# Two-layer hybrid decoder on one core: channel-mixing pieces made between steps of the u projection, the pool stage one group late, key/value sums in two banks

## The chip, the cores and the metric

The kernel runs on one core of one Trainium2 chip. The metric is the device time of one execution in microseconds (us). The kernel before took 1982.2 us in the median of three runs (1977.94 to 1982.73). One further execution was profiled; all rows of the profile are from that one.

The core has five engines with a queue each: PE does matrix products into PSUM, DVE and ACT work on SBUF and PSUM, POOL on SBUF, and SP issues the transfers (DMA). An engine takes the instructions of its queue in order and waits at one whose inputs or buffers are not ready. The program below is written for a scheduler that simulates the engines when the kernel is compiled: the order of the program is a priority, and the order in a queue can differ from it.

## The reference

```python
for l in range(DEPTH):                                   # 2 layers, x is (1, 1024, 1024)
    h = rms_norm(x, g_pre_mix[l]) * (1.0 + scale_m) + shift_m
    proj = h @ w_in[l] + b_in[l]
    q, k, v, u = jnp.split(proj, [512, 640, 768], axis=-1)
    attn_out = sliding_window_attention_with_sinks(rotary(q), rotary(k), v, sinks[l])
    pool_out = causal_pool_mixer(u, pool_w[l], pool_scale[l])
    mix = jnp.concatenate([attn_out, pool_out], axis=-1) @ w_out[l]
    x = x + gate_m * rms_norm(mix, g_post_mix[l])
    h = rms_norm(x, g_pre_ffn[l]) * (1.0 + scale_f) + shift_f
    f = (jax.nn.silu(h @ w_gate[l]) * (h @ w_up[l])) @ w_down[l]
    x = x + gate_f * rms_norm(f, g_post_ffn[l])

def causal_pool_mixer(u, ...):       # four groups of 128 channels, windows 2, 4, 8, 16
    pooled = trailing_mean(u_group, w) - u_group
    out_group = (pooled @ pool_w[group]) * pool_scale
```

The shifts, scales and gates come from a small projection of `c`. All data are float32.

## The kernel before, in words

**Numbers as two parts.** Each operand of a product is split into a rounded part hi and a rest lo (`split`, line 211: hi on ACT at L213, lo on DVE at L214), and each product is three matmuls, hi hi, hi lo, lo hi (`mm3`, line 238: L239, L242, L243). One has up to 128 x 128 x 512.

**Halves and passes.** The 1024 tokens are worked in two halves of 512 (four tiles of 128). For each half three passes read the normalised input, eight channel pieces of 128 kept transposed as hi and lo in eight `hT` buffers: `q_pass` (line 653; four PSUM banks, one per token tile), `kv_pass` (line 617; keys and values, 256 columns per token tile) and `u_pass` (line 674; the pool mixer's input, four banks, one per channel group). Each step of a pass loads a strip of `w_in` into a `raw` buffer (`weight`, line 216), splits it and issues twelve products (of 256 columns in `kv_pass`, which loads one strip for two k). When a pass ends, its banks are emptied: q on DVE (L672), key/value on DVE (L651), u on ACT (L686). There are four accumulator banks (`acc`), three others (`msc`) for transposes and short products, and one for attention (`pv`).

**Pieces.** `pre_norm_piece` (line 494) makes one channel piece: four transposes of 128 x 128 on PE into an `msc` bank (L489), scale and shift on ACT into `raw` (L475), if wanted a write of that to memory (`keep`, L498, on SP's queue), then the split into an `hT` buffer.

**Rings.** `part` (line 124) hands out buffers in pieces of 512 columns: `raw` is two tiles of 2048, `hi` and `lo` three tiles of 1024 each, so four and six pieces of 512. A tile is free again only when everything that reads any of its pieces is done.

**Order of the work.** Stages are generators, and `run` (line 596) drives one of them and, after each of its steps, advances others by a share of calls:

```python
for _ in stream:
    i += 1
    for o in others:
        while o[2] * steps < o[1] * i:
            o[2] += 1
            next(o[0], None)
```

Per layer the order is: `dense0` (q and key/value of the first half); then `dense` (line 1339), 20 steps: u of the first half (8 steps, which also make the pieces of the second half), key/value of the second half (4 steps), q of the second half (8 steps), with the attention of the first half, `pool0` (line 1344: eight empty calls, then the pool stage of the first half) and a part of the small projection beside it; then the output projection of the first half (`mix_out`), which begins with the four pool groups; then `post_norm` of the first half, whose normalised rows `fn` are the input of the channel mixing; then u of the second half (line 1358) with ten calls of attention; then, at line 1362, the eight pieces of the first half for the channel mixing, each written to memory too (`kept0`, read again much later by `up_sums`); then `up_firsts` (line 1002), the first products of the channel mixing, whose weights come through `operand` (line 1009, loads at L1012), with attention and the pool stage of the second half beside it (line 1373). The first of each two matmul groups there uses the first four pieces, the second the other four.

**Pool stage.** `pool_mix` (line 890) takes one group per call: one to four doubling sums on DVE (L903), the scaled difference (L907), for the first half a correction of the first 16 columns (L912, L913), a split, three matmuls with the group's weights `pwh` and `pwl` into an `msc` bank, and the scaling on ACT into `cat` (L920).

**Key/value banks.** With `pairs` given (the very first pass of the kernel only), two token tiles share a bank; in the other three passes each of the four token tiles has a bank of its own. With two in a bank, only the first product of the first tile clears the bank, and only the last of the second closes it; `other` keeps the second tile's opening product behind the first tile's.

## Time and profile before

| what | value |
|---|---|
| median of three runs | 1982.2 us (1977.94 to 1982.73) |
| the profiled execution's own time | 1979.58 us |
| its span, first to last instruction | 1977.8 us |
| instructions | 26045 |
| mean granted clock of PE | 0.985 |
| HBM traffic over the span | 169 GB/s |

In the rows of the profile, `out<-in` names the buffers that an instruction writes and reads, `x` is a count, and times are us from the span's start. A group's row ends with busy us, the mean ns of one, and the idle time of the engine just before, with what ended it. In the timeline a row is start, length, engine, line and operation, and in brackets the idle time before it and its releaser. PEld is the loading of PE's weights, which runs beside its matmuls; SPq is the issue of a transfer. A matmul's row shows its whole latency, so rows overlap; matmuls of 256 columns start about 0.12 us apart, those of 512 columns about 0.23.

### The profile page before, as it was taken

To read this page: it belongs to the slowest core of one execution; us is meant where nothing else is said; L and a number is where in the kernel's file an instruction comes from. 1 tells how busy PE (TensorE), PEld (TensorE's weight loads), DVE (VectorE), ACT (ScalarE), POOL (GpSimd) and SP (SyncE) were. 2 spreads that over 40 slices of the span, in tenths; PEclk is the share of its full clock that TensorE was granted. 3 is DMA by queue.
4 is the path that set the end of the run, shared out by engine and by line. 5 is a ranking of instruction groups with operands and counts; after the bars stand their busy time and mean duration, and the time that the engine had idled before them with its cause. 6 is when DMAs were issued, how large, how long until landed. Compare 5 with 4: busy or idle time off the path is not lost. (4 is left out here: it accounts for less than half of the span.)

```text
span 1977.8 us, 26045 instructions
## 1 busy us (share of the span) xinstructions
PE 1891.2 (96%) x8958; PEld 1551.3 (78%) x8958; DVE 1564.9 (79%) x2907; ACT 957.1 (48%) x1794; POOL 49.7 (3%) x100
## 2 busy tenths in 40 slices
PE   6989989999999999999999899899999999999997
PEld 4877768887888887778887777788778888878886
DVE  6988976679889886787878889656788898767687
ACT  4775785653222223445648658845522222335452
POOL 1000000010000000000000000000200000000000
PEclk9999989999999999999999899899999999999999
DMA  9236553555455446842556455445555554474343
GB/s 327 88 108 187 176 192 121 160 192 192 157 180 192 161 164 229 302 129 88 178 192 182 131 146 184 135 131 189 176 192 176 175 177 170 142 262 171 112 134 112
DMA packets 222052, 336.62 MB, mean 170 GB/s; under 512 B 16696, under 2 KB 120008, under 8 KB 221920
## 3 DMA queue, kind: packets, MB, share of 16 engines
q1 hardware_dynamic: 221776, 334.92, 51.2%
q8 instruction: 70, 1.15, 0.2%
q14 instruction: 62, 0.51, 0.1%
q0 software_dynamic: 32, 0.00, 0.0%
q10 hardware_dynamic: 112, 0.04, 0.0%
HBM read 262.00 MB, written 72.89 MB: 169 GB/s over the span
## 5 line engine op out<-in xcount | busy, mean ns | idle before, releaser
L213 ACT ACTIVATE hi<-raw 128x1024 fp32r<-128x1024 f32 (+1 forms) x388 | 332.0, 867 | 335.7 <-PE acc L242 214.5
L214 DVE TENSOR_TENSOR lo<-raw,hi 128x1024 fp32r<-128x1024 f32 (+1 forms) x388 | 379.7, 984 | 80.6 <-ACT hi L213 77.1
L239 PE MATMUL acc<-t,hi 128*128 128x512 f32 x704 | 276.1, 392 | 4.9 <-ACT hi L213 4.9
L243 PE MATMUL acc<-t,lo 128*128 128x512 f32 x704 | 275.9, 393 | 3.6 <-DVE lo L214 3.6
L242 PE MATMUL acc<-t,hi 128*128 128x512 f32 x704 | 275.5, 391 | 0.0
L243 PE MATMUL acc<-bh,lo 128*128 128x512 f32 x528 | 207.1, 392 | 0.0
L239 PE MATMUL acc<-bh,hi 128*128 128x512 f32 x528 | 203.9, 391 | 3.0 <-ACT bh L213 3.0
L239 PE MATMUL acc<-hT,hi 128*128 128x512 f32 x480 | 192.0, 400 | 9.7 <-ACT hi L213 9.1
L1061 DVE TENSOR_TENSOR fn<-acc,fn 128x512 f32<-128x512 f32 x220 | 150.4, 684 | 50.9 <-PE acc L243 50.1
L242 PE MATMUL acc<-hT,hi 128*128 128x512 f32 x480 | 189.7, 395 | 0.0
L243 PE MATMUL acc<-hT,lo 128*128 128x512 f32 x480 | 187.8, 394 | 0.0
L239 PEld LDWEIGHTS acc<-t,hi 128*128 128x128 f32 x704 | 133.3, 189 | 34.1 <-ACT hi L213 6.5
L243 PEld LDWEIGHTS acc<-t,lo 128*128 128x128 f32 x704 | 133.1, 189 | 34.2 <-DVE lo L214 6.7
L242 PEld LDWEIGHTS acc<-t,hi 128*128 128x128 f32 x704 | 133.2, 189 | 27.8
L242 PE MATMUL acc<-ph,hi 128*128 128x512 f32 x320 | 126.4, 395 | 0.7 <-DVE ph L214 0.6
L239 PEld LDWEIGHTS acc<-bh,hi 128*128 128x128 f32 x528 | 99.4, 189 | 24.8 <-ACT bh L213 3.8
L273 DVE SCALAR_TENSOR_TENSOR ada<-ar,c_act,ada 128x512 f32<-128x512 f32 x140 | 104.4, 746 | 15.9 <-DMA ar<-in_ada_w_dram 14.9
L243 PEld LDWEIGHTS acc<-bh,lo 128*128 128x128 f32 x528 | 100.1, 190 | 20.7
L239 PEld LDWEIGHTS acc<-hT,hi 128*128 128x128 f32 x480 | 91.3, 190 | 29.9 <-ACT hi L213 10.8
L999 ACT ACTIVATE fn<-fn 128x512 f32<-128x512 f32 x44 | 27.8, 633 | 168.4 <-DVE fn L1061 157.9
L243 PEld LDWEIGHTS acc<-hT,lo 128*128 128x128 f32 x480 | 90.7, 189 | 18.7 <-DVE lo L214 0.4
L242 PEld LDWEIGHTS acc<-hT,hi 128*128 128x128 f32 x480 | 91.5, 191 | 17.4
(302 smaller groups left out, 3877.1 us busy)
## 6 DMA issues: line engine op xcount, KB each, us to landing
ar<-in_ada_w_dram SPq DMA_DIRECT2D x160, 256.0 KB
raw<-in_w_gate_dram SPq DMA_DIRECT2D x44, 512.0 KB
raw<-in_w_up_dram SPq DMA_DIRECT2D x44, 512.0 KB
raw<-in_w_in_dram SPq DMA_DIRECT2D x80, 256.0 KB
raw<-keeps SPq DMA_DIRECT2D x40, 512.0 KB
keeps<-fn SPq DMA_DIRECT2D x66, 256.0 KB
two_b<-in_w_down_dram SPq DMA_DIRECT2D x30, 512.0 KB
raw<-keepa SPq DMA_DIRECT2D x25, 512.0 KB
```

The lines of the kernel that those rows point to most:

```text
L213: nc.scalar.activation(hi, src, AF.Copy)
L214: nc.vector.tensor_sub(lo, src, hi.bitcast(F32))
L239: ins = nc.tensor.matmul(dst, lh, rh, start=first, stop=False)
L242: nc.tensor.matmul(dst, lh, rl, start=False, stop=False)
L243: return nc.tensor.matmul(dst, ll, rh, start=False, stop=last)
L273: nc.vector.scalar_tensor_tensor(acc, w, c_act[:, i : i + 1], acc, op0=ALU.mult, op1=ALU.add)
L999: nc.scalar.activation(g, g, AF.Silu)
L1061: nc.vector.tensor_add(halves_of(dst)[m], bank, halves_of(src)[m])
```

## The change

Three edits, all in the order of the work; no instruction's operation or size changes.

1. `kv_pass`: two accumulator banks in all passes, two token tiles to a bank, in the way that the first pass of the kernel had already.
2. `pool_mix`: the matmuls and the scaling of a group are issued in the call after the one that makes its split; the last group has a call of its own, so the stage has five calls. `pool0` gets 13 calls over the 20 steps of `dense` in place of 20: its eight empty ones come by step 11, its five working ones at steps 13, 14, 16, 17 and 19 (before: steps 9 to 12).
3. The eight pieces of the first half for the channel mixing come from a generator beside the u pass of the second half: three empty calls, then one piece per call. Five pieces are asked for behind u's steps 4 to 8, the other three behind the pass.

```diff
     def kv_pass(l, hT, par, qkvs, pairs=None):
-        if pairs:
-            dsts = [pairs[t // 2][:, t % 2 * 256 : t % 2 * 256 + 256] for t in range(NT)]
-        else:
-            dsts = [acc_bank()[:, :256] for _ in range(NT)]
+        banks = pairs or [acc_bank() for _ in range(2)]
+        dsts = [banks[t // 2][:, t % 2 * 256 : t % 2 * 256 + 256] for t in range(NT)]
...
-                first, second = pairs and t % 2 == 0, pairs and t % 2 == 1
+                first, second = t % 2 == 0, t % 2 == 1
...
-    POOL_STEPS = len(WINDOWS)
+    POOL_STEPS = len(WINDOWS) + 1
...
+        def mapped(g, hi, lo_):
+            bank = msc_bank()
+            sl = slice(g * P, (g + 1) * P)
+            mm3(bank, pwh[:, sl], pwl[:, sl], hi, lo_, True, True)
+            sc = cols[:, 8 * KD + g : 8 * KD + g + 1]
+            nc.scalar.activation(cat[:, g, :], bank, AF.Copy, scale=sc)
+
+        late = None
         for g, w in enumerate(WINDOWS):
...
             hi, lo_ = part("hi"), part("lo")
             split(hi, lo_, pooled)
-            bank = msc_bank()
-            sl = slice(g * P, (g + 1) * P)
-            mm3(bank, pwh[:, sl], pwl[:, sl], hi, lo_, True, True)
-            sc = cols[:, 8 * KD + g : 8 * KD + g + 1]
-            nc.scalar.activation(cat[:, g, :], bank, AF.Copy, scale=sc)
+            if late:
+                mapped(*late)
+            late = (g, hi, lo_)
             yield
+        mapped(*late)
+        yield
...
-        run(dense(), 2 * KD + 4, (att, ATT_STEPS + 2), (pool0(), 2 * KD + 4), (side, 16))
+        run(dense(), 2 * KD + 4, (att, ATT_STEPS + 2), (pool0(), KD + POOL_STEPS), (side, 16))
...
-        run(u_pass(l, 1, pieces, cols, uts[1], lambda k, ins: None), KD, (att, 10))
+        kept0 = dr.tile([KD, P, T], F32, tag="h0", name="h0", bufs=DEPTH)
+        hts0 = []
+
+        def first_half():
+            for _ in range(3):
+                yield
+            for k in range(KD):
+                hts0.append(pre_norm_piece(0, k, par["abf"], None, fn, kept0[k]))
+                yield
+
+        pre = first_half()
+        run(u_pass(l, 1, pieces, cols, uts[1], lambda k, ins: None), KD, (att, 10), (pre, KD))
         pool = pool_mix(l, 1, uts[1], cols, cats[1][1])
-
-        kept0 = dr.tile([KD, P, T], F32, tag="h0", name="h0", bufs=DEPTH)
-        hts0 = [pre_norm_piece(0, k, par["abf"], None, fn, kept0[k]) for k in range(KD)]
+        drain(pre)
         ops = {B11: hts0[:HK], B21: hts0[HK:]}
```

## The prediction

> **What bounds the kernel now.** I read the page first, then windows set by stage, the waits, the groups by form, and the timeline of the two places that the diff touches.

> ```profile
> span 1977.8 us, 26045 instructions
> PE 1891.2 (96%) x8958; PEld 1551.3 (78%) x8958; DVE 1564.9 (79%) x2907; ACT 957.1 (48%) x1794; POOL 49.7 (3%) x100
> ```

> PE is busy for 96% of the span, so only stretches in which PE is not full, or its clock is low, can give anything. 1977.8 - 1891.2 = 86.6 us are idle in all. The next view gives the stretches that the change touches: per stretch its length, then the busy time of PE, PEld, DVE, ACT and POOL, the granted clock, and the DMA share.

> ```profile
> core 0: us, PE busy (x) PEld busy (x) DVE busy (x) ACT busy (x) POOL busy (x), PEclk, DMA share, GB/s
> 130.00:148.00 18.00, 12.85 (x63) 9.36 (x62) 13.52 (x39) 10.07 (x25) 0.00 (x0) 0.91 0.00 1
> 148.00:178.00 30.00, 29.72 (x166) 24.92 (x166) 25.57 (x68) 16.29 (x44) 1.09 (x4) 1.00 0.64 193
> 260.00:271.50 11.50, 11.50 (x67) 9.82 (x67) 6.11 (x22) 8.78 (x22) 0.88 (x5) 1.00 0.02 5
> 271.50:288.06 16.56, 10.40 (x67) 8.17 (x65) 10.82 (x30) 14.66 (x31) 0.33 (x1) 0.88 0.67 213
> 288.06:294.30 6.24, 6.24 (x17) 4.95 (x18) 4.68 (x6) 3.73 (x7) 0.00 (x0) 0.51 0.87 266
> 310.00:320.00 10.00, 10.00 (x46) 8.24 (x45) 8.11 (x11) 4.30 (x6) 0.00 (x0) 1.00 0.48 155
> 1103.00:1124.00 21.00, 15.54 (x72) 11.56 (x71) 16.89 (x44) 10.91 (x28) 0.47 (x2) 0.83 0.43 127
> 1124.00:1156.00 32.00, 31.99 (x170) 26.90 (x169) 25.72 (x70) 16.01 (x43) 1.35 (x4) 0.95 0.47 139
> 1250.00:1266.58 16.58, 10.85 (x67) 8.46 (x65) 10.80 (x30) 14.65 (x31) 0.33 (x1) 0.81 0.66 215
> 1266.58:1270.40 3.82, 3.82 (x12) 3.04 (x13) 3.64 (x6) 3.52 (x7) 0.00 (x0) 0.50 0.79 248
> ```

> Two kinds of hole, each once per layer. I count a hole as PE's idle time plus what the low clock takes, busy x (1 - clock).
> **Hole A** lies between the u projection of the second half and the first matmul of the channel mixing: layer 0 6.16 + 10.40 x 0.12 = 7.4, then 6.24 x 0.49 = 3.1; layer 1 5.73 + 10.85 x 0.19 = 7.8, then 3.82 x 0.50 = 1.9. Together 20.2 us.
> **Hole B** lies between the key/value pass and the q pass of the second half: layer 0 5.15 + 12.85 x 0.09 = 6.3; layer 1 5.46 + 15.54 x 0.17 = 8.1. Together 14.4 us.
> So 34.6 us (1.7%) is the most that this change can take away. Behind both holes PE is full again (29.72 of 30.00, 31.99 of 32.00).

> **Hole A, the pieces.** The timeline of layer 0 in order:

> ```profile
> 251.33 0.33 SPq L223 DMA_DIRECT2D raw<-in_w_in_dram  x1
> 251.71 1.90 SPq L510 DMA_DIRECT2D cfa<-in_x_dram  x4
> 258.43 2.19 ACT L463 ACTIVATE fn<-fn,rs 128x1024 f32<-128x1024 f32 x2 [0.23 <-DVE rs L257]
> 273.17 1.04 PE L489 MATMUL msc<-ident,fn 128*128 128x128 f32 x8
> 274.66 3.36 SPq L498 DMA_DIRECT2D h<-raw  x4
> 280.57 0.38 SPq L1012 DMA_DIRECT2D raw<-in_w_gate_dram  x1
> 282.81 0.46 SPq L1012 DMA_DIRECT2D raw<-in_w_up_dram  x1
> 286.95 1.06 ACT L213 ACTIVATE hi<-raw 128x1024 fp32r<-128x1024 f32 x1 [0.96 <-DMA raw<-in_w_up_dram]
> 288.06 0.80 PE L239 MATMUL acc<-hT,hi 128*128 128x512 f32 x1 [1.70 <-ACT hi L213]
> ```

> The groups by form in 271.50 to 288.06 (count | busy us, mean ns of one | idle before):

> ```profile
> L475 ACT ACTIVATE raw<-msc,colp 128x512 f32<-128x512 f32 x8 | 5.8, 790 | 0.0
> L214 DVE TENSOR_TENSOR hT<-raw,hT 128x512 fp32r<-128x512 f32 x8 | 5.2, 688 | 3.3 <-ACT hT L213 3.3
> L213 ACT ACTIVATE hT<-raw 128x512 fp32r<-128x512 f32 x8 | 4.7, 649 | 0.0
> ```

> The normalised rows are there at 258.43 + 2.19 = 260.6, yet the first transpose runs at 273.17: in program order all eight pieces stand behind the u pass. Then ACT paces them, 0.79 + 0.65 = 1.44 us a piece, 11.5 for eight; it is busy 14.66 of 16.56 us. The last link is a transfer: the first weights of the channel mixing are issued at 280.57 and 282.81, since their buffer (the `raw` ring, two tiles of 2048) has to be given back by the first four pieces' keep writes, which start at 274.66. They are there at 286.95, and PE starts at 288.06.

> What the change does here: per layer 32 transposes (0.13 us each, 1.04 / 8), 16 ACT operations, 8 DVE operations and 8 keep writes on SP's queue move, none is added. Three of u's eight steps pass before the first piece, five pieces are made behind steps 4 to 8, three behind the pass. Nothing can start before 260.6, so the pieces get the last 11 us of the u pass. The 20 transposes put 20 x 0.13 = 2.6 us into a stretch where PE is full (11.50 of 11.50); they delay u by that and leave the hole by the same amount: 0. DVE has room for 8 x 0.69 = 5.5 (6.11 of 11.50 busy): 0. ACT is the limit: it has 11.50 - 8.78 = 2.7 us free ahead of 271.5 and 16.56 - 14.66 = 1.9 behind it. If all ACT work that stands ahead of the first weight split stays ahead of it, that split moves up by at most 4.6 us. If it overtakes the four pieces that only the second matmul group needs (4 x 1.44 = 5.8), the transfer decides, and the whole 7.4 could go. Below nothing: ACT's attention work may be pushed back by a piece at each step (1.44 x 5 = 7.2 lost), which I leave at the end of the bounds because ACT's free time covers most of it. I take 4.6 per layer, 9.2 for both; layer 1 has the same ACT figure (14.65 of 16.58).
> The clock's part of the hole is 1.25 + 3.06 + 2.06 + 1.91 = 8.3 us. No row shows the clock with a shorter hole; its ends are 0 and 8.3, and I take half, 4.1. Hole A gives **13.3**.
> [...]

> The queue that the pieces are moved past is SP's: the keep of piece 0 now stands in program order ahead of u's weight loads 4 to 7, that of piece 1 ahead of 5 to 7, and so on. I cost that at 0, because the queue's order is not the program's: the last load of u's weights went out at 251.33 and the second half's residual, which the program asks for only after the whole next stage, at 251.71, both long before the first keep (274.66). The scheduler sends a load as soon as its buffer is free. What it costs if that cover is gone is the third rival.

> **Hole B, the pool stage and the banks.**

> ```profile
> 129.80 0.28 PE L242 MATMUL acc<-lo,hT 128*128 128x256 f32 x1
> 129.92 0.28 PE L243 MATMUL acc<-hi,hT 128*128 128x256 f32 x1
> 132.11 0.51 PE L239 MATMUL msc<-hi,pwh 128*128 128x512 f32 x1 [1.91 <-ACT hi L213]
> 137.90 0.69 DVE L903 TENSOR_TENSOR pt<-pt 128x513 f32<-128x513 f32 x1
> 138.50 0.42 DVE L651 TENSOR_TENSOR qkv<-acc,bqkv 128x256 f32<-128x256 f32 x1
> 138.97 0.50 PE L239 MATMUL acc<-hi,hT 128*128 128x512 f32 x1 [1.29 <-DVE qkv L651]
> 140.17 0.50 PE L242 MATMUL acc<-lo,hT 128*128 128x512 f32 x1 [0.69 <-DVE lo L214]
> ```

> The pool stage's groups by form in 104 to 148:

> ```profile
> L903 DVE TENSOR_TENSOR pt<-uT 128x527 f32<-128x527 f32 x4 | 2.8, 697 | 0.0
> L214 DVE TENSOR_TENSOR lo<-pt,hi 128x512 fp32r<-128x512 f32 x4 | 2.7, 686 | 1.0 <-ACT hi L213 1.0
> L907 DVE SCALAR_TENSOR_TENSOR pt<-pt,uT 128x512 f32<-128x512 f32 x4 | 2.7, 682 | 0.0
> ```

> The key/value pass ends at 129.92. PE then waits 1.91 us for a pool group's split, and at 138.97 for the last key/value eviction (L651), which stands behind the pool sums in DVE's line; at 140.17 for a weight split on the same engine. All three waits are DVE's backlog. The pool stage is ten doubling sums (1 + 2 + 3 + 4 by the loop) of about 0.70, four of 0.68 and four splits of 0.69: 12.5 us of DVE.
> The change moves it from steps 9 to 12 of this run, on top of the key/value pass, to steps 13, 14, 16, 17 and 19, inside the q pass (13 calls over 20 steps, the first eight empty); maps each group one call later, so that PE meets a split made a call ago; and leaves two banks free in the key/value pass, so that the first two of four token tiles of q need no eviction at all. Instructions are the same in number.
> The DVE work does not go away. PE's hole closes only as far as DVE works in what are now its own pauses: 18.00 - 13.52 = 4.5 and 21.00 - 16.89 = 4.1 us in the two holes, 8.6 together, while the upper end is the whole hole, 14.4. The q pass behind has DVE pauses of 4.4 (30.00 - 25.57) and 6.3 (32.00 - 25.72), so 12.5 us of pool work fit only with the hole's own time; that is why I stay at DVE's figure, **8.6**. The lower end: a pool group's hi and lo halves are held a call longer in a ring of six halves, so a weight split can wait as at 132.11, 1.91 at each of eight groups, 15.3 lost. I take 0 for it, since about four halves are asked for between two calls (one for a weight at each step, three for attention in four).
> The third key/value pass (layer 1, first half) and the pool stage of the second half: 0. The first waits for q's first bank either way; the second lies under the channel mixing's matmuls, where PE is full (10.00 of 10.00 from 310), and would cost one 1.91 a group if that cover were gone.
> [...]

> **Sum.** 9.2 + 4.1 + 8.6 = 21.9 us off the profiled execution's 1979.6 (span 1977.8 and 1.8 around it): 1957.7. That execution lies 2.6 below the median of the runs, 1982.2, so the forecast against the runs is **1960**.

> **Rivals.** All against 1982.2; 0.3% (5.9 us) is about what a measurement of this kernel can tell from no change.
> *Only one hole closes.* For it: both holes have a second limiter close behind (ACT 14.66 of 16.56; DVE 25.57 of 30.00). Hole A alone gives 1969, hole B alone 1974. Chance 0.21.
> *Hidden anyway, no change.* The pieces cannot start before 260.6, and if the scheduler already orders ACT by readiness, the first weight split may stay where it is, while hole B moves with the pool sums into the q pass and opens there. Holes return elsewhere: 1979 to 1985. Chance 0.14.
> *Keeps ahead of weight loads, slower.* If the schedule keeps the new program order on SP, a load of u's weights waits for a keep, the keep for ACT, ACT for the transposes, and these for the u step before. Then each step shows a load (282.81 to 286.95, 4.1 us) and a split (1.06): 5.2 us of bare PE, four steps a layer, 41.6 in all, 1982.2 - 21.9 + 41.6 = 2002. It decides from three steps a layer on (31.2 against 21.9); with one or two caught the change still wins. Against it stand the rows at 251.33 and 251.71. Chance 0.10.
> The forecast keeps 0.55. Faster: 0.55 + 0.21 = 0.76; within 0.3%: 0.14; slower: 0.10.
> **Range.** Both holes gone in full gives 1982.2 - 34.6 = 1947.6; hole B at its lower end with hole A as forecast gives 1982.2 - 13.3 + 15.3 = 1984. I take 1947 to 1983, which leaves out the slow rival and little else; the likeliest case's own range is 1948 to 1972.

> **What would show it.** Right: transposes `msc<-ident,fn` between u's matmuls from about 11 us ahead of u's end; fewer than 16.6 us from u's last matmul to the first of the channel mixing, about 12; the clock above 0.9 there; no L651 ahead of q's first matmul; pool matmuls among q's, with no wait on a split. Wrong: `raw<-in_w_in` issues behind `h<-raw` and PE waiting on `hi` inside the u pass (the slow rival); a DVE wait of the same length later in the q pass or at the start of the output projection (hidden anyway).

## The result and the profile after

The changed kernel takes **1947.07 us** in the median of four runs (1944.55 to 1948.14), against 1981.39 (1977.94 to 1982.73) for the kernel before: a ratio of 0.9828 with a 95% interval of 0.9811 to 0.9845, or 34 us less. The forecast was 1960 in a range of 1947 to 1983. The sign and the places were right; the gain was 34 us where 22 were forecast. The median lies 0.07 us inside the lower end of the range, and two of the four runs lie below it, so that it fell inside is luck. The profiled execution took 1944.55 us (before 1979.58), at a mean granted clock of 0.993 (before 0.985).

The head of the page after the change:

```profile
span 1942.8 us, 26040 instructions
PE 1874.0 (96%) x8958; PEld 1541.0 (79%) x8958; DVE 1564.3 (81%) x2907; ACT 954.5 (49%) x1794; POOL 49.0 (3%) x100
```

DVE's work is the same to 0.6 us (1564.9 before), and PE has the same 8958 matmuls: no work was taken away. PE is idle for 68.8 us instead of 86.6, and its same matmuls are busy for 17.2 us less, most of which is the clock (1891.2 x 0.015 = 28.4 us lost to it before, 1874.0 x 0.007 = 13.1 after). The windows by stage of the changed kernel (length, then busy time of PE, PEld, DVE, ACT and POOL, the clock, DMA), the counterparts of the ones in the prediction:

```profile
126.30:144.30 18.00, 18.00 (x114) 15.32 (x113) 16.82 (x51) 12.09 (x30) 0.47 (x2) 1.00 0.35 111
144.30:170.00 25.70, 23.36 (x125) 18.76 (x124) 25.04 (x66) 15.65 (x42) 1.14 (x4) 1.00 0.48 146
252.40:269.90 17.50, 17.46 (x111) 14.94 (x111) 12.02 (x38) 15.55 (x34) 0.89 (x5) 1.00 0.42 148
269.90:275.37 5.47, 3.47 (x27) 2.86 (x25) 4.10 (x12) 5.47 (x10) 0.00 (x0) 0.97 0.82 249
275.37:281.60 6.23, 6.23 (x28) 5.30 (x29) 4.62 (x12) 5.35 (x17) 0.33 (x1) 0.75 0.71 232
1083.90:1101.00 17.10, 16.86 (x104) 14.34 (x104) 16.54 (x50) 10.30 (x26) 0.41 (x2) 1.00 0.58 162
1226.50:1231.90 5.40, 3.40 (x27) 2.79 (x25) 4.02 (x12) 5.40 (x10) 0.00 (x0) 1.00 0.87 266
1231.90:1236.00 4.10, 4.10 (x22) 3.40 (x23) 3.71 (x10) 4.10 (x14) 0.33 (x1) 1.00 0.51 178
```

Hole B is gone: the 18 us behind the key/value pass hold 18.00 us of PE work at full clock, where they held 12.85 at 0.91. Hole A is 5.5 us long in both layers where it was 16.8, and of these PE is idle for 2.0. By the prediction's own count (idle time plus what the clock takes), hole A fell from 20.2 us to 2.00 + 0.10 + 1.56 in layer 0 and 2.00 in layer 1, 5.7 in all, and hole B from 14.4 to 0.2. Not all of that is gain: from the key/value pass to q's end PE was idle for 7.5 + 5.5 us before and is still idle for 3.3 + 1.9, now mostly within the q pass (rows below).

The waits of PE in layer 0's key/value and q passes (104 to 180 us), the two longest of each, first before, then after (us in total, times, longest):

```profile
PE msc L239 <- ACT hi L213: 1.9, 1, 1.9
PE acc L239 <- DVE qkv L651: 1.3, 1, 1.3
```

```profile
PE acc L242 <- DVE lo L214: 1.9, 2, 1.5
PE msc L737 <- DVE rt L705: 1.3, 1, 1.3
```

The wait for a pool group's split and that for the last key/value eviction (L651, which is L649 now) are gone. Two other waits on DVE are the longest now: on weight splits inside the q pass (1.46 us ahead of 150.23 and 0.42 ahead of 158.05), and on L705 behind it (1.33 ahead of 174.10).

What is left of hole A, in the timeline of the changed kernel:

```profile
267.89 0.38 SPq L1019 DMA_DIRECT2D raw<-in_w_gate_dram  x1
268.88 0.43 SPq L1019 DMA_DIRECT2D raw<-in_w_up_dram  x1
270.14 1.25 PE L489 MATMUL msc<-ident,fn 128*128 128x128 f32 x10
272.24 2.47 SPq L498 DMA_DIRECT2D h<-raw  x3
274.22 1.09 ACT L213 ACTIVATE hi<-raw 128x1024 fp32r<-128x1024 f32 x1
275.37 0.80 PE L239 MATMUL acc<-hT,hi 128*128 128x512 f32 x1 [2.00 <-ACT hi L213]
```

Of the 32 transposes only ten run behind the u pass (before: all 32; 22 run inside it now, the first of them 17.4 us ahead of its end), and the first weights of the channel mixing are issued at 267.89, 2.0 us before the u pass's last matmul (269.91), where it was 9.3 us behind it. The first weight split at 274.22 has no wait of its own ahead of it in this view; ACT is busy for 5.47 of 5.47 us.

Stage by stage, from the first and last matmuls of each in the two traces: from the key/value pass's first to q's last matmul 69.84 to 61.58 in layer 0 and 68.14 to 59.05 in layer 1 (17.4 saved); from u's first matmul to the channel mixing's first 47.75 to 41.09 and 47.74 to 41.07 (13.3 saved); layer 0's channel mixing 2.7 saved; the third key/value pass (layer 1, first half) 13.71 to 11.39 (2.3 saved); all else 0.6 lost. The sum is the 35.0 us by which the span is shorter.

### The profile page after: what moved, and what is told of

Read it like the earlier page. It is cut to its first block, busy times and chain, and to the rows that moved or that the text cites. A ratio compares the mean times of both kernels' runs of the same rounds, so it can differ in the third digit from the quotient of the medians.

```text
span 1942.8 us, 26040 instructions
## 1 busy us (share of the span) xinstructions
PE 1874.0 (96%) x8958; PEld 1541.0 (79%) x8958; DVE 1564.3 (81%) x2907; ACT 954.5 (49%) x1794; POOL 49.0 (3%) x100
## 5 line engine op out<-in xcount | busy, mean ns | idle before, releaser
L213 ACT ACTIVATE hi<-raw 128x1024 fp32r<-128x1024 f32 (+1 forms) x388 | 332.5, 869 | 377.8 <-PE acc L242 220.7
L214 DVE TENSOR_TENSOR lo<-raw,hi 128x1024 fp32r<-128x1024 f32 (+1 forms) x388 | 382.9, 993 | 113.4 <-ACT hi L213 112.6
L239 PE MATMUL acc<-t,hi 128*128 128x512 f32 x704 | 276.7, 393 | 5.7 <-ACT hi L213 5.7
L243 PE MATMUL acc<-t,lo 128*128 128x512 f32 x704 | 276.1, 393 | 3.4 <-DVE lo L214 3.4
L242 PE MATMUL acc<-t,hi 128*128 128x512 f32 x704 | 276.0, 392 | 0.0
L243 PE MATMUL acc<-bh,lo 128*128 128x512 f32 x528 | 206.4, 391 | 0.0
L239 PE MATMUL acc<-bh,hi 128*128 128x512 f32 x528 | 203.5, 390 | 3.0 <-ACT bh L213 3.0
L239 PE MATMUL acc<-hT,hi 128*128 128x512 f32 x480 | 191.2, 398 | 7.8 <-ACT hi L213 7.2
L242 PE MATMUL acc<-hT,hi 128*128 128x512 f32 x480 | 188.3, 392 | 0.0
L243 PE MATMUL acc<-hT,lo 128*128 128x512 f32 x480 | 186.8, 393 | 0.9 <-DVE lo L214 0.9
L239 PEld LDWEIGHTS acc<-t,hi 128*128 128x128 f32 x704 | 133.5, 190 | 34.9 <-ACT hi L213 7.3
L243 PEld LDWEIGHTS acc<-t,lo 128*128 128x128 f32 x704 | 133.4, 190 | 34.2 <-DVE lo L214 6.5
L242 PEld LDWEIGHTS acc<-t,hi 128*128 128x128 f32 x704 | 133.5, 190 | 27.9
L242 PE MATMUL acc<-ph,hi 128*128 128x512 f32 x320 | 126.0, 394 | 1.3 <-DVE ph L214 1.1
L239 PEld LDWEIGHTS acc<-bh,hi 128*128 128x128 f32 x528 | 99.1, 188 | 24.6 <-ACT bh L213 3.8
L273 DVE SCALAR_TENSOR_TENSOR ada<-ar,c_act,ada 128x512 f32<-128x512 f32 x140 | 104.7, 748 | 17.0 <-DMA ar<-in_ada_w_dram 15.8
L243 PEld LDWEIGHTS acc<-bh,lo 128*128 128x128 f32 x528 | 99.6, 189 | 20.5
L239 PEld LDWEIGHTS acc<-hT,hi 128*128 128x128 f32 x480 | 90.7, 189 | 27.4 <-ACT hi L213 9.1
L243 PEld LDWEIGHTS acc<-hT,lo 128*128 128x128 f32 x480 | 90.1, 188 | 19.5 <-DVE lo L214 1.3
L242 PEld LDWEIGHTS acc<-hT,hi 128*128 128x128 f32 x480 | 90.7, 189 | 17.3 <-issue 0.2
```

Source lines behind the costliest of these rows:

```text
L213: nc.scalar.activation(hi, src, AF.Copy)
L214: nc.vector.tensor_sub(lo, src, hi.bitcast(F32))
L239: ins = nc.tensor.matmul(dst, lh, rh, start=first, stop=False)
L242: nc.tensor.matmul(dst, lh, rl, start=False, stop=False)
L243: return nc.tensor.matmul(dst, ll, rh, start=False, stop=last)
L273: nc.vector.scalar_tensor_tensor(acc, w, c_act[:, i : i + 1], acc, op0=ALU.mult, op1=ALU.add)
```

## The experiments

Each ratio is against the kernel before, run on the same chip, with its 95% interval. The expectations write TensorE for PE, VectorE for DVE and ScalarE for ACT. The lengths in the table are from each kernel's trace, in us: "kv to q" from the second half's first key/value matmul to the last of q, "u to mixing" from u's first matmul to the channel mixing's first, in layers 0 and 1, and "hole" its last part, behind u's last matmul.

| kernel | median | ratio | kv to q | u to mixing | hole | third kv pass |
|---|---|---|---|---|---|---|
| before | | | 69.84, 68.14 | 47.75, 47.74 | 16.76, 16.79 | 13.71 |
| after | 1947.07 | 0.9828 | 61.58, 59.05 | 41.09, 41.07 | 5.45, 5.47 | 11.39 |
| pieces alone | 1966.11 | 0.9928 [0.9908, 0.9949] | 67.44, 68.04 | 41.08, 41.07 | 5.48, 5.46 | 13.22 |
| pool alone | 1962.35 | 0.9907 [0.9885, 0.9929] | 62.98, 58.73 | 47.13, 47.49 | 16.08, 16.54 | 12.74 |
| banks alone | 1972.36 | 0.9963 [0.9949, 0.9977] | 70.16, 63.87 | 47.72, 47.19 | 16.69, 16.23 | 11.41 |
| pool and banks | 1959.52 | 0.9895 [0.9873, 0.9917] | 61.53, 58.82 | 47.77, 47.28 | 16.82, 16.32 | 11.39 |
| pool: later calls only | 1968.30 | 0.9931 [0.9910, 0.9952] | 58.58, 57.87 | 47.58, 47.63 | 16.67, 16.71 | 13.28 |
| pool: lag only | 1977.78 | 0.9985 [0.9972, 0.9999] | 72.93, 63.37 | 47.34, 47.62 | 16.32, 16.68 | 12.85 |
| six sums left out | 1966.08 | 0.9932 [0.9915, 0.9950] | 63.10, 59.51 | 47.41, 47.36 | 16.41, 16.36 | 12.87 |
| matmuls among transposes | 1981.85 | 1.0007 [0.9994, 1.0020] | 69.89, 67.36 | 48.00, 50.13 | 17.06, 19.20 | 15.10 |
| before, other row buffers | 1961.89 | 0.9913 [0.9889, 0.9937] | 67.74, 66.52 | 37.06, 36.64 | 5.65, 5.65 | 14.86 |
| after, other row buffers | 1943.60 | 0.9812 [0.9787, 0.9836] | 61.36, 58.82 | 35.46, 35.68 | 2.66, 2.65 | 11.39 |
| after, loads behind keeps | 1960.33 | 0.9898 [0.9877, 0.9918] | 63.78, 60.40 | 43.82, 44.15 | 1.43, 1.42 | 11.40 |
| after, weights first | 1942.50 | 0.9810 [0.9785, 0.9836] | 61.96, 58.85 | 36.88, 36.87 | 1.24, 1.25 | 11.39 |

**The three edits by themselves.** The first kernel is the one before with the pieces' generator, the second with the pool stage's lag and its 13 calls, the third with the two banks, the fourth with pool stage and banks; each takes its lines of the diff above as they are.

> The kernel before with the channel pieces' edit alone. By the milestones of the two traces (from the end of the q pass to the first products of the channel mixing, and the stretch behind it) this edit is worth 5.3 + 2.7 us in layer 0 and 7.6 + 0.3 in layer 1. Theory 1, the two holes are separate and add up: 15 to 17 us faster than before (ratio about 0.992), the first channel-mixing matmul about 5.5 us behind u's last instead of 16.8 in both layers, and nothing changed between the key/value pass and the q pass. Rival, the gain behind u is partly a gain of the stages before, handed on: under 10 us.

> The kernel before with the pool stage's edit alone (first half's calls at steps 13 to 19, mapping one call late); key/value products keep four banks. Theory 1, the hole before q is VectorE's backlog of pool sums: 13 to 17 us faster, the matmul of the first pool group moves behind q's first, and the wait on L651 in layer 0 shrinks since the eviction no longer stands behind pool sums. Rival, the hole is the wait for the key/value evictions because the q pass needs the same banks: under 6 us faster, PE still waits for a key/value eviction after the key/value pass.

> The kernel before with the two banks' edit alone. Theory 1 (backlog): the two free banks let q's first steps start while the pool sums still hold VectorE, but the weight splits are in the same line, so 2 to 6 us faster, of which 2.3 in the first half's pass of layer 1. Rival (evictions): 10 us or more faster. Second rival, sharing a bank makes the first tile's eviction wait for the second's matmuls: 0 to 1 us slower.

> The kernel before with the pool stage's and the two banks' edits, without the pieces'. Theory 1, the holes add up: 18 to 20 us faster, so that with the pieces' edit alone it makes up the 34.3 us of the whole change within 3. Rival, pool stage and banks remove the same wait: no more than the better one of the two alone. Second rival, they need each other: more than the sum of the two alone by over 3 us.

Pieces alone give 0.72%, 14.3 us, a little under the expected 15 to 17, and pool with banks 1.05%, 20.8 us; together that is 35.1, the 34.1 of the whole change within the intervals. So the gains at the two holes are separate and add up. (Against expectation kv to q, which the pieces don't touch, is 2.4 us shorter in layer 0 with them, though only 0.1 in layer 1; untouched stages shift by such amounts between these kernels, and no cause is claimed for them.) Inside hole B the pool stage does most (18.4 us alone, above the 13 to 17 expected). Pool stage and banks don't add up: alone they give 18.4 + 7.3 = 25.7, together 20.8. That is 2.4 more than the pool stage alone, with overlapping intervals, so the times don't tell it from the rival by which both remove the same wait; the third key/value pass, 12.74 with the pool stage and 11.39 with both, is where the traces show the banks. The banks alone gave 7.3 us, above the 2 to 6 expected and below the rival's 10, though the interval (4.6 to 10.1) touches both. Their timeline in layer 0 shows why they don't open hole B by themselves:

```profile
132.16 0.51 PE L239 MATMUL msc<-hi,pwh 128*128 128x512 f32 x1 [2.36 <-ACT hi L213]
140.00 0.50 PE L239 MATMUL acc<-hi,hT 128*128 128x512 f32 x1 [1.29 <-DVE qkv L649]
141.21 0.50 PE L242 MATMUL acc<-lo,hT 128*128 128x512 f32 x1 [0.70 <-DVE lo L214]
```

The same three waits as before: q's last token tile still needs the last eviction, and that still stands behind the pool sums in DVE's line. What the banks gave lies in the third key/value pass (2.3 us, in every kernel that has the edit) and in layer 1 from key/value to q (4.3 us). The windows of that q pass, behind q's fifth matmul, before and with the banks alone:

```profile
1114.83:1153.51 38.68, 37.08 (x184) 30.72 (x185) 28.75 (x77) 22.92 (x61) 1.35 (x4) 0.89 0.48 141
```

```profile
1114.41:1148.03 33.62, 33.42 (x182) 27.70 (x181) 27.88 (x75) 20.16 (x56) 0.86 (x4) 0.97 0.53 158
```

37.08 x 0.11 = 4.1 us went to the low clock before, 33.42 x 0.03 = 1.0 here: some 3 us of that stage's gain are the clock, which fell behind the hole in one and barely in the other.

**Which half of the pool edit.** The fifth kernel has only the later calls, the sixth only the lag:

```diff
-        run(dense(), 2 * KD + 4, (att, ATT_STEPS + 2), (pool0(), 2 * KD + 4), (side, 16))
+        run(dense(), 2 * KD + 4, (att, ATT_STEPS + 2), (pool0(), KD + POOL_STEPS), (side, 16))
```

```diff
-            bank = msc_bank()
...
+            if late:
+                mapped(*late)
+            late = (g, hi, lo_)
             yield
+        mapped(*late)
+        yield
```

> The kernel before, and of the pool stage's edit only the later calls: 12 calls over the 20 steps, so the stage starts at step 13 instead of 9; each group is still mapped in its own call. Theory 1, the hole before q is VectorE's backlog and closes because the pool sums leave the key/value pass: 13 to 17 us faster, almost all of the 18.2 that the whole pool edit gave, the fifth matmul of q about 7 us earlier in each layer. Rival, the call's lag is what counts (TensorE no longer meets a split that has just been asked for): under 6 us faster, with waits of about 1.9 us on a pool group's split inside the q pass.

> The kernel before, and of the pool stage's edit only the lag: each group mapped one call after its sums, the calls where they were (steps 9 to 12, the last mapping at step 13). Theory 1 (backlog): 0 to 5 us faster, at most the two waits of 1.9 on a pool group's split per layer; q's fifth matmul moves by under 3 us per layer. Rival (the lag is what counts): 10 us or more.

The later calls alone give 0.69%, 13.7 us, the lag alone 0.15%, 3 us. It is the place of the sums that counts. The lag seems to have its worth on top, some 5 us by intervals that overlap, at another place: with the later calls alone kv to q is even shorter (58.58, 57.87), but from q's last to u's first matmul it takes 67.55 and 69.34 us against 63.24 and 65.33 before; with the lag too that stretch is 63.52 and 64.61. The likely reason: 12 calls over 20 steps put the groups at steps 14, 16, 17 and 19 (not from 13 on, as expected), 13 calls at 13, 14, 16 and 17, so that less of the pool stage is left for the output projection, which needs it first. That was not tried by itself.

**Is it DVE's backlog?** The seventh kernel makes the queue shorter and moves nothing:

```diff
-            while width < w:
+            while width < 2:
```

> The kernel before with six of the ten doubling sums of each pool stage left out (each group makes one; the wider pooling windows are thereby not computed). Nothing else moves. Theory 1 (backlog): six sums of 0.70 us are 4.2 us less VectorE work in front of the weight splits and evictions, so q's fifth matmul comes 3.5 to 4.5 us earlier in each layer, 7 to 9 us in all; the second half's stage, under a full TensorE, gives 0. Rival (evictions or banks, not backlog): under 2 us in all.

0.68%, 13.5 us, nearly twice the 7 to 9 expected, and far from the rival's 2. Key/value to q, one row per layer, before, after, and with the six sums left out:

```profile
107.24:177.08 69.84, 62.34 (x379) 52.32 (x377) 59.50 (x163) 42.90 (x112) 2.29 (x8) 0.98 0.44 134
1085.37:1153.51 68.14, 62.66 (x371) 53.42 (x370) 57.18 (x155) 40.17 (x105) 2.35 (x7) 0.92 0.43 130
```

```profile
108.08:169.66 61.58, 58.30 (x379) 50.45 (x377) 58.66 (x163) 42.41 (x112) 2.35 (x8) 1.00 0.49 152
1067.37:1126.42 59.05, 57.20 (x372) 50.02 (x371) 56.04 (x156) 39.62 (x105) 2.10 (x7) 1.00 0.47 141
```

```profile
107.56:170.66 63.10, 60.32 (x378) 51.11 (x377) 55.76 (x157) 42.80 (x112) 2.19 (x8) 1.00 0.49 147
1079.92:1139.43 59.51, 58.25 (x372) 49.83 (x370) 53.67 (x150) 39.28 (x105) 2.12 (x7) 1.00 0.50 151
```

Read the fourth number, DVE. Left out were 3.7 and 3.5 us of it, and the stretches are 6.7 and 8.6 us shorter. Most of the rest is what a hole costs besides itself: before, the clock took 62.34 x 0.02 + 62.66 x 0.08 = 6.3 us here, and it is whole in both other kernels. In the changed kernel DVE does nearly the same work as before (114.7 us against 116.7), and it is its pauses that went: 69.84 - 59.50 + 68.14 - 57.18 = 21.3 us before, 2.9 + 3.0 = 5.9 after. That is 15.4 of the 17.4 us. Every stretch is an engine's work plus its pauses; that DVE is the engine to count here is what this kernel shows, which takes only DVE work away, together with the fifth, which only moves it. In the changed kernel DVE is busy for 95% of both stretches, and PE for 95 and 97%.

**The clock in hole A.** The eighth kernel asks what the clock does when PE is kept busy there: it adds four ordinary matmuls per piece into the bank that the transposes then overwrite:

```diff
+            bank = msc_bank()
+            hot = pieces[KD - 1][0]
+            for _ in range(4):
+                nc.tensor.matmul(bank, ident_r, hot if k < KD - 1 else hts0[0][0], start=True, stop=True)
+            transposed(0, k, None, fn, bank)
```

> The kernel before with 32 more ordinary 128x512 matmuls per layer, four ahead of each piece's four transposes, into the bank that these then overwrite (0.23 us each, 7.4 us per layer, in a stretch where TensorE is idle for 6 us). [...]

Over 289.50 to 295.70 us, the first 6.2 us of the channel mixing, the clock is 0.72, where before it was 0.51 over the first 6.24, and the time lies between 1.2 us less and 4.0 more. Its windows in layer 0:

```profile
274.00:285.06 11.06, 11.06 (x68) 9.25 (x67) 5.26 (x11) 9.67 (x15) 0.00 (x0) 1.00 0.50 174
286.90:289.40 2.50, 0.03 (x2) 0.01 (x1) 0.87 (x4) 1.11 (x2) 0.00 (x0) 1.00 1.09 375
290.88:294.80 3.92, 3.92 (x17) 3.45 (x17) 2.19 (x9) 2.76 (x10) 0.33 (x1) 0.58 0.80 236
```

With PE full (11.06 of 11.06 us) the clock is 1.00 through all the pieces. Then comes a bare wait of 2.5 us for the first weights, and it falls all the same, to 0.58 some 1.5 us into the products. The time is no shorter; the hole ends behind the same transfer, and in layer 1 it is even 2.4 us longer. What the transposes alone do is not told by this kernel, whose added matmuls filled the pauses too; the trace of the kernel before tells more. Its stretches of halved clock start whole multiples of 3.41 us apart, and last 3.41, 6.83 or 10.24 us but for the one that ends the trace. These are three slots of that length in hole A, counted on from those starts, then the pieces' transposes alone (L489; busy time of PE and PEld) in the first:

```profile
277.15:280.56 3.41, 2.34 (x15) 1.62 (x16) 1.29 (x2) 3.41 (x7) 0.00 (x0) 1.00 0.70 234
280.56:283.97 3.41, 0.94 (x7) 0.50 (x5) 3.30 (x10) 3.41 (x9) 0.00 (x0) 1.00 0.99 329
283.97:287.39 3.42, 2.02 (x6) 1.43 (x6) 2.48 (x9) 2.46 (x10) 0.33 (x1) 0.50 0.96 266
```

```profile
277.15:280.56 3.41, 1.88 (x12) 1.17 (x12) 1.00 0.70 234
```

The first slot has 2.34 us of PE work, of which 1.88 are transposes, and the clock behind it stays at 1.00. The second has 0.94 us (0.66 of it transposes of the attention, L816), and behind it the clock is 0.50. In the traces of the kernel before and of the changed one, between the first 20 and the last 15 us, every slot at full clock with under 1.45 us of PE work (seven, 0.32 to 1.43 us) is followed by a halved one. Without the transposes of L489 four slots of the trace before would be under 1.45 too: from 24.56, 273.73, 277.15 and 1253.36 us on PE is busy for 1.96, 2.88, 2.34 and 3.15 us, of which 1.09, 2.09, 1.88 and 2.55 are these transposes, and no fall is behind any of them. So transposes counted in these slots, and the fall in hole A of layer 0 came behind the slot in which PE had least to do.

**What ends hole A.** The ninth and tenth kernels take each piece's row buffer from rings that are idle there, the ninth on the kernel before (all else as it was, the pieces behind the u pass), the tenth on the changed one:

```diff
-        hts0 = [pre_norm_piece(0, k, par["abf"], None, fn, kept0[k]) for k in range(KD)]
+        hts0 = [pre_norm_piece(0, k, par["abf"], None, fn, kept0[k], t_("ada", [P, T]) if k % 3 == 2 else t_("ar", [P, T])) for k in range(KD)]
```

> The kernel before, in which each piece's row buffer is taken from rings that are idle there instead of the ring `raw`, so that the first weights of the channel mixing need not wait for the keep writes. Theory 1 (the prediction's reading of hole A): the transfer is the last link, but ScalarE stands close behind it with 1.9 us free, so the first channel-mixing matmul comes 1 to 2 us earlier in each layer, 2 to 4 us in all. Rival (the transfer decides alone): the weights land some 6 us earlier and the hole shortens by 4 us or more a layer, over 8 in all. Second rival, ScalarE's pieces decide: under 1 us in all.

> The changed kernel with the same other buffers for the pieces' rows. Theory 1: after the change ScalarE fills the remaining hole of 5.5 us without a pause and no transfer is waited for, so nothing changes: within 2 us of the changed kernel's 1947.1, hole 5 to 6 us. Rival (the keeps still hold the weights back): the hole falls below 4 us in both layers and the time to 1943 or less.

Both fell to the rival, the ninth by far: 0.87%, 17.2 us, and "u to mixing" is 10.7 and 11.1 us shorter with no piece moved; the tenth by its hole, 2.66 and 2.65, while its median, 1943.6, just misses the rival's 1943. The ninth's timeline:

```profile
250.46 0.43 SPq L1012 DMA_DIRECT2D raw<-in_w_gate_dram  x1
250.94 0.50 SPq L1012 DMA_DIRECT2D raw<-in_w_up_dram  x1
266.49 1.06 ACT L213 ACTIVATE hi<-raw 128x1024 fp32r<-128x1024 f32 x1
272.31 1.04 PE L489 MATMUL msc<-ident,fn 128*128 128x128 f32 x8
276.10 0.39 PE L239 MATMUL acc<-hT,hi 128*128 128x512 f32 x1
```

The first weights go out at 250.46, 20 us ahead of u's last matmul (270.45), for the ring `raw` is not taken by pieces that wait to be written. Their split runs at 266.49, still inside the u pass and ahead of all eight pieces on ACT; the first products need four pieces only, and the last three are made under them. PE is idle in the hole for 0.40 and 0.41 us, and in layer 0 the clock is 1.00 behind it (276.10 to 282.00 us). This is what the prediction put aside as "if it overtakes". In the tenth kernel the u pass is 32.8 us instead of 35.6 and the hole 2.66 instead of 5.45, with no idle time left in it. Part of that is other work at the place: 16 transposes run in its u pass instead of 22, and eight behind the first products instead of none.

**The slow rival made true.** In the eleventh kernel each of u's weight loads 4 to 7 is held on SP's queue behind the keep of the piece that is asked for just before it:

```diff
-            nc.sync.dma_start(dst, src)
+            ins = nc.sync.dma_start(dst, src)
+            if kept_ins:
+                after(ins, kept_ins.pop())
...
-            nc.sync.dma_start(keep, hf)
+            kept_ins.append(nc.sync.dma_start(keep, hf))
```

> The changed kernel with the slow rival made true: each of u's weight loads 4 to 7 of the second half is held on SP's queue behind the keep write of the piece that the program asks for just before it. The prediction's price: 5.2 us of bare TensorE a step, four steps in each of two layers, 41.6 us, so about 1989, which is slower than the kernel before (ratio about 1.004). Rival price: the loads have a step's time of u's matmuls (3.5 us) to hide under and weights ahead in their ring, so only part of each is bare, 1 to 3 us a step, 8 to 24 us in all: 1955 to 1971, still faster than before.

Slower than the changed kernel by 13.3 us, and still faster than the one before: the rival price holds, 1.7 us a step by the whole time. Two of the holds, and the one wait over 1 us on a weight split that the u pass of layer 0 shows for them:

```profile
254.05 0.33 SPq L502 DMA_DIRECT2D h<-raw  x1
254.42 0.43 SPq L225 DMA_DIRECT2D raw<-in_w_in_dram  x1
258.99 0.33 SPq L502 DMA_DIRECT2D h<-raw  x1
259.41 0.38 SPq L225 DMA_DIRECT2D raw<-in_w_in_dram  x1
262.92 0.50 PE L243 MATMUL acc<-hT,hi 128*128 128x512 f32 x1 [1.06 <-ACT hi L213]
```

The u pass grows by 6.8 and 7.1 us, and 4.0 of that comes back in each layer, since the hole behind it shrinks to 1.4. All 32 transposes run in that u pass, and PE is idle in it for 4.6 and 5.0 us instead of 1.35 and 1.3. So 5.8 of the 13.3 us lie at the place itself, 0.7 a step; the rest lies in other stages (above all 4.6 in layer 0's channel mixing and 3.6 in kv to q), and its cause stays open.

**A version that may beat both.** In the twelfth kernel the changed one asks for the first weights ahead of the last three pieces:

```diff
-        drain(pre)
-        ops = {B11: hts0[:HK], B21: hts0[HK:]}
+        ops = {}
...
-        run(firsts[0], 1 + 2 * FIRST[0], (att, ATT_STEPS), (pool, POOL_STEPS))
+        next(firsts[0])
+        drain(pre)
+        ops.update({B11: hts0[:HK], B21: hts0[HK:]})
+        run(firsts[0], 2 * FIRST[0], (att, ATT_STEPS), (pool, POOL_STEPS))
```

> The changed kernel with the first weight group of the channel mixing asked for ahead of the last three pieces, which only the second group's matmuls need. Theory 1 (what is left of hole A is ScalarE's line: the first weight split stands behind the last pieces, 1.44 us each): the first channel-mixing matmul follows u's last by 1 to 3.5 us instead of 5.5, 4 to 8 us faster than the changed kernel in all (1939 to 1943). Rival (the first weights land too late, or the pieces' own matmuls then wait): within 2 us of 1947.1, the same wait a few matmuls later.

The hole is 1.24 us, all of it PE work, and the median 1942.5, as expected. Its issues come 4.7 and 5.3 us earlier than the changed kernel's, since they take their `raw` buffers ahead of the last three pieces:

```profile
263.16 0.42 SPq L1019 DMA_DIRECT2D raw<-in_w_gate_dram  x1
263.63 0.68 SPq L1019 DMA_DIRECT2D raw<-in_w_up_dram  x1
268.13 1.06 ACT L213 ACTIVATE hi<-raw 128x1024 fp32r<-128x1024 f32 x1
```

Both this and the tenth kernel lie 3 to 4 us below the changed one by their ratios, but their intervals overlap with its, so a gain is not shown. The traces say why it is small: "u to mixing" is shorter by 8.4 us in this kernel and by 11.0 in the tenth, both layers together, but some 8 us of either come back in the channel mixing behind it (5.5 and 4.3 in layer 0), and the span of this kernel's profiled execution is only 0.8 us shorter than the changed kernel's. Of the 5.45 us of hole PE was idle for 2.0; the rest was attention and transposes that have to run somewhere.

## Why the prediction was right, and where its sizes were off

**Reading of the bounds: right in the main.** The holes were the two places, DVE's line was the cause of hole B, and PE's work did not change. But the 34.6 us called "the most that this change can take away" were not the most: the span is 35.0 us shorter, though some 6 us of the two holes' count are left. The sum of 21.9 us was two thirds of the 34 measured; one term, hole B, was half its size, and the two of hole A missed by less, one above and one below.

**Hole B, 8.6 forecast, 17.4 measured: the failed term.** The step was "DVE works in what are now its own pauses", with the pauses of the hole alone, on the ground that 12.5 us of pool work would not fit into the q pass. Three things were wrong. The pauses were counted from 148 and 1124 on (4.4 and 6.3); over the whole q pass, from q's fifth matmul, they are 36.91 - 28.20 = 8.7 in layer 0, by this row,

```profile
140.17:177.08 36.91, 35.38 (x187) 28.90 (x187) 28.20 (x79) 22.52 (x61) 1.09 (x4) 0.95 0.51 153
```

and 38.68 - 28.75 = 9.9 in layer 1 (the row stands above). From the key/value pass to q's end there were 21.3 us of pauses, and 15.4 of them went. The pool sums did open the q pass a little, as feared (25.70 - 23.36 = 2.3 us of idle PE from 144.30 on), but the hole gave 5.2 in layer 0 and the clock besides. The row that should have carried the term is one per layer from the key/value pass to q's end, for that is where the moved work could go.

And the term had nothing in it for the clock. By PE's side of the same rows the 17.4 us are 7.8 of idle time (13.0 to 5.1) and 9.5 of busy time for the same matmuls (125.0 to 115.5), of which 6.3 are the low clock; what the other 3 are stays open. The prediction's own windows held 12.85 x 0.09 + 15.54 x 0.17 = 3.8 us of clock, and it took "PE is full again" from 1124:1156, where the clock of 0.95 took another 31.99 x 0.05 = 1.6. That is part of why the measured 17.4 are more than the 14.4 that were called the whole hole.

**Hole A, 13.3 forecast, about 14.5 measured.** By the prediction's count 14.5 of 20.2 us went, and the edit alone gave 14.3. The parts: idle time 7.9 (9.2 forecast from ACT's free time), clock 6.6 of 8.3 (half, 4.1, forecast). The total came out by luck, from one part too high and one too low, and by a reason that was not right: ACT was taken as the limit and the transfer as the last link close behind. The ninth kernel shows that the limit was the `raw` ring. Once the weights land early their split overtakes the pieces on ACT, and the whole hole goes (0.4 us of idle left in each layer) without any move. The moved pieces probably helped by giving the ring back earlier: in layer 0 the first keep goes out 14.5 us ahead of u's end where it was 3.4 behind it, and the first weights 2.0 ahead where they were 9.3 behind. That ACT had the pieces off its line as well was not told apart from this. The sign "about 12" us for the hole came out as 5.5, while the u pass grew by 4.6.

**The 20 transposes in the u pass.** They were 22, and they began 17.4 us ahead of u's end, not about 11: "nothing can start before 260.6" did not hold, as the last of the normalised rows are there 15.8 us ahead of u's end in the changed kernel (254.1 against 269.91) where they were there 10.7 ahead. The price of 0.13 each is fair: with the other row buffers 16 run there, and the u pass is 1.8 and 2.1 us longer than before. In the changed kernel it is 4.6 longer, because 14 matmuls of attention have moved into it too; its idle time is what it was (1.3 and 1.35 us).

**The clock.** The 4.1 us were half of what the low clock took in hole A, as no row showed the clock with a shorter hole. In layer 0 of the trace before, behind a slot made mostly of transposes (1.88 of 2.34 us) it stayed at 1.00, and it fell to 0.50 behind the next one, in which PE was busy for 0.94 of 3.41 us and idle for 2.47.

**The third key/value pass, 0 forecast, 2.3 measured.** It did not wait for q's first bank "either way": before, PE waited 1.9 us in it for q's evictions (DVE L672), and the changed kernel has no such wait there. No loss from two token tiles in one bank shows in that pass: each kernel with the edit has it 1.3 us or more shorter than any without.

**The rivals.** "Only one hole closes" is what the first and fourth kernels are made to be: 1966 and 1960 against its 1969 and 1974. "Hidden anyway" was held off by DVE's pauses, as far as the rows above show. "Keeps ahead of weight loads" happened in order only: in the changed kernel the last load of u's weights goes out at 262.48, behind two keeps (255.39 and 260.17), but PE waits for no weight split in the u pass. Its price was wrong as well: 41.6 us forecast, 13.3 measured. A held load has most of a u step to hide under: in the eleventh kernel PE's longest wait on a split in the u pass is 1.06 us in layer 0 and 1.4 in layer 1 where the price had 5.2, and that kernel stays faster than the one before.

## What to carry to other kernels

When work moves off a busy engine's line, count that engine's pauses over every stage to which the work can go, not only in the hole that it leaves; and price the low clock with the hole. Before moving the producers of a late stage, look at which buffer its first load is waiting for: here a ring shared with rows waiting to be written held hole A, and taking those rows from another ring gave as much as moving the pieces did. A hole's length is not what closing it gives; its idle time, with the clock lost behind it, is.

## What the runs showed of the hardware

Behind the same stall the clock is halved once and not another time. Hole A of the changed kernel, in layer 0 and in layer 1: first the stall, then the slots of 3.41 us around it, counted from the starts of that trace's halved stretches.

```profile
273.10:275.37 2.27, 0.27 (x4) 0.04 (x2) 1.96 (x9) 2.27 (x5) 0.00 (x0) 0.93 0.78 253
271.66:275.07 3.41, 1.71 (x12) 1.20 (x11) 2.48 (x9) 3.41 (x6) 0.00 (x0) 1.00 0.79 229
275.07:278.49 3.42, 3.12 (x8) 2.55 (x9) 2.76 (x4) 3.42 (x13) 0.00 (x0) 0.50 0.57 219
1229.63:1231.90 2.27, 0.28 (x4) 0.04 (x2) 1.96 (x9) 2.27 (x5) 0.00 (x0) 1.00 0.90 291
1227.39:1230.80 3.41, 2.51 (x19) 1.99 (x17) 2.38 (x8) 3.41 (x7) 0.00 (x0) 1.00 0.79 207
1230.80:1234.22 3.42, 2.32 (x10) 1.75 (x11) 3.11 (x6) 3.42 (x11) 0.00 (x0) 1.00 0.71 270
```

Both stalls are 2.27 us long with 0.27 and 0.28 us of PE work in them. In layer 0 nearly all of it lies in one slot, which is left with 1.71 us of PE work, and the next slot runs at half clock and loses 3.12 x 0.50 = 1.6 us. In layer 1 the stall is cut by a slot's border, both slots keep over 2.3 us of work (2.51 and 2.32), the clock is 1.00 in both and behind them, and nothing is lost to it.
